# Hybrid decoder layer: the low part of the attention scores on 64-row halves of the array, two key chunks at a time

## The chip, the cores and the metric

The kernel runs on one core of a Trainium2 chip. The metric is the device time of that core in microseconds (us), from several executions of the same program. The lower it is, the better.

## The reference, cut to what matters

The program computes one decoder layer for 2048 tokens of width 1024 in float32. An input norm is followed by one wide projection into queries, keys and values of 4 heads, a convolution branch and two gates. Each head has two query and key vectors of 64 elements per token, and a value of 128. The part that the change touches is the differential attention:

```python
s = jnp.einsum('bhmqd,bhmkd->bhmqk', qb, k).astype(jnp.float32) * scale
s = jnp.where(mask, s, -jnp.inf)
probs = jax.nn.softmax(s, axis=-1)
a = probs[:, :, 0] - lam * probs[:, :, 1]
return jnp.einsum('bhqk,bhkv->bhqv', a.astype(v.dtype), v)
```

After it come the branch outputs, a gated merge, a mixture of 32 experts with two experts per token, and a per-layer embedding. All of these are large matrix products.

## The kernel before, in words

**Number format.** Every operand of a large product is split into a high and a low part (`split`, lines 90 to 93): ScalarE (ACT) rounds the value to the short format, VectorE (DVE) or GpSimd (POOL) subtracts. Ordinary products then take three matmuls, high x high, high x low and low x high (`mm3`, lines 95 to 99). Attention scores are built otherwise. The depth of a score is only 64, so the 128 rows of the array carry the keys' high part in rows 0 to 63 and their low part in rows 64 to 127 (`Kt`, lines 518 to 520), and the query's high part twice, once for each half (`Qt`, slot 2m). One matmul of 128 rows thus gives q-high times (k-high + k-low), and a second one, with the query's low part twice (slot 2m + 1), gives q-low times (k-high + k-low).

**Stages.** `mix` makes the projections and writes q, k, v, gates and the convolution result to scratch in HBM. `attn` follows, then `merge`, `moe` and `ple`. `attn` takes 4 heads times 8 groups of 256 queries. For each group `attn_probs` makes the probabilities, and `attn_out` of the group before multiplies them with the values. Twelve gate columns of `mix` (`mix_gate`, 24 groups of 24 matmuls) are written after the attention in the program, so the scheduler, which orders each engine's instructions by priority at build time, uses them to fill holes of TensorE (PE) in the attention.

**One group of scores.** For each of the two tiles of 128 queries (`qi`) and each of the two softmaxes (`m`) the keys come in chunks of 512. A group g has (2g + 4) // 4 chunks, so 1, 1, 2, 2, 3, 3, 4, 4 for g = 0 to 7. The last chunk is as wide as the causal mask lets it be, at least 256 columns. Per chunk the program takes one of four PSUM banks (`sc`), issues the high matmul (line 582) and the low matmul (line 583), for the last chunk a bf16 matmul that adds the mask (line 585), and then lets DVE find the negative maximum (line 586). ACT takes the exponential (line 572), either chunk by chunk or, where `common` says so, after the maximum over all chunks is known. The probabilities go to tiles `pr` of a ring of `PR_BUFS` = 11 (line 39), a tile for each chunk and query tile, which are released when `attn_out` has transposed them (line 632).

**Loads.** SP's queue brings, at a head's first group, the two `Kt` tiles (lines 519 and 520), the group's `Qt` (lines 526 and 527), and `Vt` (line 530). `Kt` has two buffers, one for each m, so a new head's load waits until the last score of the old head has read them. The gate weights come on the same queue.

**A place elsewhere that the prediction uses.** In `moe`, a block with at most 64 rows of an expert transposes its hidden tile with a stationary operand of 64 rows, and a block with more with one of 128 rows (`turn`, line 1177). Around it stand the products of lines 1131, 1133, 1146 and 1147; those of line 1131 have 64 columns in their stationary operand.

Of the kernel before, what the change touches and what calls it, by code (L numbers as in the profile page):

```python
# [9 lines left out]
F32 = mybir.dt.float32  # L10
# [27 lines left out]
GATES_LATE = 12  # L38
PR_BUFS = 11
QK_AFTER = 10  # L40
# [31 lines left out]
def f32(ap):  # L72
    return ap.bitcast(F32)
# [10 lines left out]
class K:  # L84
# [3 lines left out]

# [1 line left out]
    def split(self, hi, lo, x, lo_eng=None):  # L90
# [43 lines left out]
    def keep(self):  # L134
        """What lasts from the merge to the end."""
        cp = self.ctx.enter_context(self.tc.tile_pool(name="keep", bufs=1, reuse_waits="tile"))
        self.gl = cp.tile([P, NT, NG], F32, name="gl")
        self.nc.vector.memset(self.base, 0.0)
        self.dst = cp.tile([P, NBLK * NE], I32, name="dst")
        self.idx = cp.tile([P, NBLK * NE], I32, name="idx")  # L140
        self.slots = cp.tile([1, 3, NE], I32, name="slots")
        self.xp = self.ctx.enter_context(self.tc.tile_pool(name="xp", bufs=2, reuse_waits="tile"))

    def consts(self, cp):
        nc, A = self.nc, self.A
        cst = cp.tile([P, 4, P], F32, name="cst")
        self.pvt = cp.tile([P, NPV], F32, name="pvt")
        self.bc = cp.tile([P, 36 + 4 * HD], F32, name="bc")
        self.tokm = cp.tile([P, 2 * NT + 1], F32, name="tokm")
        self.maskb = cp.tile([P, P], BF16, name="maskb")  # L150
        self.identb = cp.tile([P, P], BF16, name="identb")
        self.trib = cp.tile([P, P], BF16, name="trib")
        self.ident = cst[:, 0, :]
        self.iota = cst[:, 3, :]
        self.zero = cst[:, 1, :]
        self.base, self.wt, self.tops = (cst[:, 2, a:b] for a, b in ((0, NE), (NE, 2 * NE), (2 * NE, 2 * NE + 3 * NT)))
        self.wt = self.wt.rearrange("p (t k) -> p t k", k=2)
        self.tops = self.tops.rearrange("p (k t) -> p k t", k=3)
        self.onesb = cp.tile([P, P], BF16, name="onesb")
        nc.vector.memset(self.onesb, 1.0)  # L160
        self.st = cp.tile([P, H, NT], F32, name="st")
        self.neglam = cp.tile([P, 1], F32, name="neglam")
        self.s0 = cp.tile([P, H, NT], F32, name="s0")
        self.ones1 = cp.tile([P, 1], F32, name="ones1")
        nc.vector.memset(self.ones1, 1.0)
        self.eps = cp.tile([P, 1], F32, name="eps")
        nc.vector.memset(self.eps, EPS)
        self.qg8 = cp.tile([P, 1], F32, name="qg8")
        # brings in the table of the square root
        nc.scalar.activation(self.neglam, self.ones1, AF.Sqrt)  # L170

        def late():
            nc.sync.dma_start(cst, A["cst"])
            nc.sync.dma_start(self.pvt, A["pv"])
            for to, i in ((self.maskb, 1), (self.identb, 0), (self.trib, 2)):
                nc.vector.tensor_copy(to, cst[:, i, :])
            nc.vector.tensor_scalar_mul(self.qg8, self.pv("qg"), 1.0 / math.sqrt(HD))
            nc.vector.memset(self.zero, 0.0)
            nc.gpsimd.dma_start(self.bc, A["bc"])
            nc.gpsimd.dma_start(self.tokm, A["tokm"])  # L180

        self.late_consts = late

    def rstd(self, pool, ss, shape, n, tag, bufs=None):
        """1 / sqrt(ss / n + eps)."""
        nc = self.nc
# [4 lines left out]

# [1 line left out]
    def mix(self):  # L193
# [109 lines left out]
    def after(self, us, f):  # L303
        """Puts f into the program once the tensor engine has got that much other work."""
        self.todo.append([us, f])
# [18 lines left out]
    def mix_u(self, t0, n, raw=None, also=()):  # L324
        """The normed input of 512 tokens, channels on the partitions, in two parts; raw: where its channels
        may lie; also: what comes between its loads."""
        nc, A, sp, px = self.nc, self.A, self.sp, self.px
# [163 lines left out]

# [1 line left out]
    def attn(self):  # L493
        tc, nc = self.tc, self.nc
        with ExitStack() as ctx:
# [16 lines left out]
            def probs(h, g):  # L512
                if g == 0:
                    self.Kt = []
                    for m in range(2):
                        ms = slice(m * HD, (m + 1) * HD)
                        kt = kp.tile([P, S], F32R, name="Kt", tag="K")
                        for cs in (slice(0, 512), slice(512, S)):
                            nc.sync.dma_start(f32(kt[:HD, cs]), f32(self.KH[h, ms, cs]))
                            nc.sync.dma_start(f32(kt[HD:, cs]), f32(self.KL[h, ms, cs]))  # L520
                        self.Kt.append(kt)
                Qt = kp.tile([P, 4, 256], F32R, name="Qt", tag="Q")
                for l, src in enumerate((self.QH, self.QL)):
# [29 lines left out]
    def attn_probs(self, h, g, Qt, Kt):  # L553
        """Unnormalized p0 - lam * (sum p0 / sum p1) * p1; what is missing, 1 / sum p0, goes into s0."""
        nc, sp = self.nc, self.asp
# [6 lines left out]
        for qi in range(2):  # L562
# [4 lines left out]
            for m in range(2):  # L567
# [7 lines left out]

                for c, w in enumerate(ws):
                    n = max(w, 256)
                    last = c == nch - 1
                    sc = self.pS.tile([P, 512], F32, name="sc", tag="sc")
                    scs.append(sc)  # L580
                    ks = Kt[m][:, c * 512 : c * 512 + n]
                    nc.tensor.matmul(sc[:, :n], Qt[:, 2 * m, qs], ks, start=True, stop=False)
                    nc.tensor.matmul(sc[:, :n], Qt[:, 2 * m + 1, qs], ks, start=False, stop=not last)  # L583
                    if last:
                        nc.tensor.matmul(sc[:, w - P : w], self.identb, self.maskb, start=False, stop=True)
                    nc.vector.tensor_reduce(nm[:, qi, m, c : c + 1], sc[:, :w], AX.X, ALU.max, negate=True)  # L586
                    if not common[m]:
                        exps([c], nm[:, qi, m, c : c + 1])
                if common[m]:
# [57 lines left out]

# [1 line left out]
    def merge(self):  # L649
# [165 lines left out]

# [1 line left out]
    def route(self, q, L):  # L817
# [12 lines left out]
        def first(vals, top, k):  # L830
            """One-hot of the first place that holds the maximum."""
            c, o, i = new(4, k), new(4, k), new(4)
# [57 lines left out]

# [1 line left out]
    def pick(self):  # L892
# [49 lines left out]

# [1 line left out]
    def projected(self, t, pt, w, pool, tag, o):  # L944
        """Tile t of it, from units of [128, 1024] in two parts."""
        for n in range(2):
# [8 lines left out]
    def project(self, parts):  # L955
        """The first half of the tiles, while the table is made."""
        for t, tag in zip(range(0, 8, 2), ("bch", "bcl") * 2):
# [4 lines left out]

# [1 line left out]
    def moe(self):  # L964
# [115 lines left out]
    def unit(self, src, lo_eng=None, after=None):  # L1080
        """A [128, 1024] piece of a weight matrix in two parts."""
        nc = self.nc
# [17 lines left out]
    def turned(self, x, more=False, into=None):  # L1100
        """The transpose of a [128, 1024] tile in two parts, [128, 8, 128] each; `more`: the high part of 64 rows
        once again, right before their low part."""
        nc = self.nc
# [23 lines left out]
    def both(self, ps, x, w, start, stop):  # L1127
        """At most 64 rows: their two parts side by side against the weights' high part."""
        if start:
# [9 lines left out]
    def products(self, w, xt, f, ps, g, i):  # L1139
        """Half of the rows' products with w1 and w3: i = 0, the rows' high part; i = 1, their low part."""  # L1140
        for k in range(4 * g, 4 * g + 4):
# [81 lines left out]
    def weights(self):  # L1223
        """What each of a token's two experts weighs."""
        nc = self.nc
# [11 lines left out]

# [1 line left out]
    def ple(self):  # L1239
# [62 lines left out]
def layout(inputs):  # L1302
    """The inputs as the program reads them: reordered and repeated, never changed."""
    a = {k: np.asarray(v)[0] for k, v in inputs.items()}
# [71 lines left out]
```

## Time and profile before

| | |
|---|---|
| Median of three runs | 2953.11 us |
| The three runs | 2961.81, 2952.98, 2953.11 us |
| Span of the profiled execution | 2960.1 us |
| Time of the profiled execution | 2961.81 us, the only one of the three that is not shorter than the span |
| PE busy | 2736.7 us, 92% of the span |
| DVE, ACT, POOL busy | 69%, 50%, 24% |
| Attention, from its first score to the last | 718 to 1200 us of the span |

The span goes from the first to the last instruction. Some 1.7 us lie around it. Busy times of PE are modelled: a matmul of 512 columns is drawn 0.39 to 0.40 us long, though the next one starts 0.23 us later, so costs of matmuls are read from start to start. PEld is the load of the stationary operand, which can run under the matmul before. "128*128" in a row is rows times columns of the stationary operand, and the shape behind it is that of the moving operand (partitions x columns).

### The profile page before, as it was taken

The page shows a single profiled execution, that of the slowest core. Times are in us where ns is not written, and L with a number is a line of the kernel's source. Part 1 is how long each engine was busy: PE and PEld are TensorE (multiplying, and loading weights), DVE is VectorE, ACT ScalarE, POOL GpSimd, SP SyncE. Part 2 cuts the span into 40 slices and gives each one's busy share as a digit, 9 for nine tenths or more (in the row PEclk, how much of TensorE's full clock was granted, in tenths as well). Part 3 has the DMA queues.
Part 4 walks back from the last instruction along what each step waited for, and adds up shares of the span by engine and source line. Part 5 has one row for each costly group of instructions (what it writes and reads, how often), then busy time and mean ns, then how long its engine had stood idle before and what let it go on. Part 6 is the DMA issues. An engine that isn't in the chain of part 4 may idle for free. (4 is left out here: it accounts for less than half of the span.)

```text
span 2960.1 us, 40065 instructions
## 1 busy us (share of the span) xinstructions
PE 2736.7 (92%) x14078; PEld 2282.7 (77%) x14078; DVE 2041.7 (69%) x2860; ACT 1474.9 (50%) x2712; POOL 722.3 (24%) x463
## 2 busy tenths in 40 slices
PE   7999999999999999999999989898888989888988
PEld 5888877997778788787898867676666767666776
DVE  6995249995878888657567456666667777776564
ACT  4233352335766667544444345555455656565443
POOL 2021130123111000001101134544335444452122
PEclk9999999999999999999999989999999999999999
DMA  5134443235243331456556366777767776876371
GB/s 189 60 107 142 159 147 104 93 114 196 81 132 89 104 112 53 160 184 214 168 170 206 122 238 243 265 287 259 252 223 274 276 283 236 293 274 244 125 246 56
DMA packets 180220, 531.52 MB, mean 180 GB/s; under 512 B 19185, under 2 KB 48641, under 8 KB 179361
## 3 DMA queue, kind: packets, MB, share of 16 engines
q1 hardware_dynamic: 135536, 397.02, 39.9%
q0 software_dynamic: 25904, 92.45, 8.5%
q10 hardware_dynamic: 18432, 37.76, 3.4%
q8 instruction: 177, 2.90, 0.4%
q14 instruction: 171, 1.39, 0.1%
HBM read 424.66 MB, written 102.50 MB: 178 GB/s over the span
## 5 line engine op out<-in xcount | busy, mean ns | idle before, releaser
L93 DVE TENSOR_TENSOR ewl<-eraw,ewh 128x1024 fp32r<-128x1024 f32 x365 | 597.2, 1665 | 94.4 <-ACT ewh L92 88.5
L92 ACT ACTIVATE ewh<-eraw 128x1024 fp32r<-128x1024 f32 x464 | 474.1, 1065 | 54.0 <-PE mps L98 24.9
L387 DVE SCALAR_TENSOR_TENSOR co<-cb,pvt,co 128x1024 f32<-128x1024 f32 x240 | 313.6, 1345 | 1.6
L93 POOL TENSOR_TENSOR ewl<-eraw,ewh 128x1024 fp32r<-128x1024 f32 x99 | 253.8, 2563 | 185.4 <-ACT ewh L92 183.0
L1146 PE MATMUL ups<-ewh,xt 128*128 128x512 f32 x592 | 250.0, 422 | 40.3 <-issue 38.6
L1147 PE MATMUL ups<-ewl,xt 128*128 128x512 f32 x592 | 244.5, 413 | 0.9 <-DVE ewl L93 0.5
L97 PE MATMUL ps<-uh,wh 128*128 128x512 f32 x576 | 232.0, 405 | 4.4 <-ACT uh L92 4.4
L586 DVE TENSOR_REDUCE nm<-sc 128x1 f32<-128x512 f32 (+3 forms) x320 | 185.3, 606 | 66.1 <-PE sc L583 51.6
L98 PE MATMUL ps<-ul,wh 128*128 128x512 f32 x576 | 227.9, 397 | 1.1 <-POOL ul L93 1.1
L99 PE MATMUL ps<-uh,wl 128*128 128x512 f32 x576 | 227.2, 396 | 0.0
L1146 PEld LDWEIGHTS ups<-ewh,xt 128*128 128x128 f32 x592 | 119.0, 201 | 71.9 <-issue 46.0
L97 PE MATMUL ps<-wh,uh 128*128 128x384 f32 x512 | 173.0, 338 | 0.0
L99 PE MATMUL ps<-wh,ul 128*128 128x384 f32 x512 | 172.1, 336 | 0.0
L98 PE MATMUL ps<-wl,uh 128*128 128x384 f32 x512 | 172.0, 336 | 0.0
L1144 PE MATMUL ups<-ewh,xt 128*128 128x512 f32 x592 | 167.5, 406 | 3.7 <-issue 3.7
L97 PE MATMUL mps<-ewh,mh 128*128 128x256 f32 x512 | 150.3, 294 | 4.1 <-ACT mh L92 4.1
L403 POOL DMA_DIRECT2D G<-sg x64 | 35.1, 549 | 457.3 <-ACT sg L402 325.2
L98 PE MATMUL mps<-ewl,mh 128*128 128x256 f32 x512 | 145.8, 285 | 0.0
L99 PE MATMUL mps<-ewh,ml 128*128 128x256 f32 x512 | 145.2, 285 | 0.0
L1147 PEld LDWEIGHTS ups<-ewl,xt 128*128 128x128 f32 x592 | 119.3, 202 | 25.5 <-DVE ewl L93 1.0
L430 POOL TENSOR_TENSOR qn<-qk,qk_std 128x1024 f32<-128x1024 f32 x16 | 44.6, 2785 | 380.7 <-DVE qk_std L189 363.8
L1204 POOL DMA_INDIRECT Y<-y,dst x48 | 72.3, 1507 | 266.3 <-POOLq L1034 188.3
(340 smaller groups left out, 7238.5 us busy)
## 6 DMA issues: line engine op xcount, KB each, us to landing
eraw<-in_we SPq DMA_DIRECT2D x384, 512.0 KB, 7.3
G<-sg POOLq DMA_DIRECT2D x64, 256.0 KB, 2.7
eraw<-in_wac SPq DMA_DIRECT2D x32, 512.0 KB, 4.3
ga<-G SPq DMA_DIRECT2D x32, 512.0 KB, 5.1
eraw<-in_wo SPq DMA_DIRECT2D x32, 512.0 KB, 3.7
ys<-Y SPq DMA_DIRECT2D x32, 512.0 KB, 8.2
wraw<-in_wqkv SPq DMA_DIRECT2D x16, 768.0 KB, 4.2
wraw<-in_wg SPq DMA_DIRECT2D x20, 512.0 KB, 3.9
```

The source lines that it names most:

```text
L92: nc.scalar.activation(hi, x, AF.Copy)
L93: (lo_eng or nc.vector).tensor_tensor(lo, x, f32(hi), ALU.subtract)
L97: nc.tensor.matmul(ps, lh, rh, start=start, stop=False)
L98: nc.tensor.matmul(ps, lh, rl, start=False, stop=False)
L99: nc.tensor.matmul(ps, ll, rh, start=False, stop=stop)
L387: nc.vector.scalar_tensor_tensor(acc, cb[:, i : i + HALF], wi, acc, ALU.mult, ALU.add)
L430: nc.gpsimd.tensor_tensor(qn.rearrange("p t (s d) -> p t s d", d=HD), qk.rearrange("p t (s d) -> p t s d", d=HD), r.unsqueeze(3).to_broadc ...
L586: nc.vector.tensor_reduce(nm[:, qi, m, c : c + 1], sc[:, :w], AX.X, ALU.max, negate=True)
L1144: self.nc.tensor.matmul(ps, xt[1][:, k, :], wk[0], start=False, stop=k == NK - 1)
L1146: self.nc.tensor.matmul(ps, xt[0][:, k, :], wk[0], start=k == 0, stop=False)
L1147: self.nc.tensor.matmul(ps, xt[0][:, k, :], wk[1], start=False, stop=False)
L1204: nc.gpsimd.indirect_dma_start(out=self.Y[:, :], out_offset=bass.IndirectOffsetOnAxis(ap=dst[R], axis=0), in_=y[R], in_offset=None)
```

## The change

The low matmul takes only the keys' high part. It then needs 64 rows, and two chunks are issued as a pair, one on rows 0 to 63 and one on rows 64 to 127. For that the high parts must lie in the other half too: for m = 1 the two halves of `Kt` change places, and a third tile `Kx` holds the high part of m = 0 in rows 64 to 127 and that of m = 1 in rows 0 to 63. `Kx` is loaded by two transfers of 512 KB at each head's start, behind `Kt` and ahead of `Qt`, into one buffer. Its 8 KB per partition are those of two `pr` tiles, so the ring has 9. The order for a pair is now: both high matmuls, both low matmuls, then mask and maxima. A chunk without a partner keeps a low matmul of 128 rows.

```diff
-PR_BUFS = 11
+PR_BUFS = 9
...
                         for cs in (slice(0, 512), slice(512, S)):
-                            nc.sync.dma_start(f32(kt[:HD, cs]), f32(self.KH[h, ms, cs]))
-                            nc.sync.dma_start(f32(kt[HD:, cs]), f32(self.KL[h, ms, cs]))
+                            for r, src in zip((slice(0, HD), slice(HD, P)), (self.KH, self.KL)[:: 1 - 2 * m]):
+                                nc.sync.dma_start(f32(kt[r, cs]), f32(src[h, ms, cs]))
                         self.Kt.append(kt)
+                    kx = kp.tile([P, S], F32R, name="Kx", tag="Kx", bufs=1)
+                    for m in range(2):
+                        nc.sync.dma_start(f32(kx[(1 - m) * HD : (2 - m) * HD]), f32(self.KH[h, m * HD : (m + 1) * HD]))
+                    self.Kt.append([(self.Kt[0], kx), (kx, self.Kt[1])])
...
-                for c, w in enumerate(ws):
-                    n = max(w, 256)
-                    last = c == nch - 1
-                    sc = self.pS.tile([P, 512], F32, name="sc", tag="sc")
-                    scs.append(sc)
-                    ks = Kt[m][:, c * 512 : c * 512 + n]
-                    nc.tensor.matmul(sc[:, :n], Qt[:, 2 * m, qs], ks, start=True, stop=False)
-                    nc.tensor.matmul(sc[:, :n], Qt[:, 2 * m + 1, qs], ks, start=False, stop=not last)
-                    if last:
-                        nc.tensor.matmul(sc[:, w - P : w], self.identb, self.maskb, start=False, stop=True)
-                    nc.vector.tensor_reduce(nm[:, qi, m, c : c + 1], sc[:, :w], AX.X, ALU.max, negate=True)
-                    if not common[m]:
-                        exps([c], nm[:, qi, m, c : c + 1])
+                ns = [max(w, 256) for w in ws]
+                for c0 in range(0, nch, 2):
+                    pair = range(c0, min(c0 + 2, nch))
+                    for c in pair:
+                        n = ns[c]
+                        sc = self.pS.tile([P, 512], F32, name="sc", tag="sc")
+                        scs.append(sc)
+                        nc.tensor.matmul(sc[:, :n], Qt[:, 2 * m, qs], Kt[m][:, c * 512 : c * 512 + n], start=True, stop=False)
+                    for c in pair:
+                        n, r = ns[c], slice(c % 2 * HD, c % 2 * HD + HD)
+                        if len(pair) == 1:
+                            r, ks = slice(0, P), Kt[m]
+                        else:
+                            ks = Kt[2][m][c % 2]
+                        nc.tensor.matmul(scs[c][:, :n], Qt[r, 2 * m + 1, qs], ks[r, c * 512 : c * 512 + n], start=False, stop=c < nch - 1)
+                    for c in pair:
+                        w, sc = ws[c], scs[c]
+                        if c == nch - 1:
+                            nc.tensor.matmul(sc[:, w - P : w], self.identb, self.maskb, start=False, stop=True)
+                        nc.vector.tensor_reduce(nm[:, qi, m, c : c + 1], sc[:, :w], AX.X, ALU.max, negate=True)
+                        if not common[m]:
+                            exps([c], nm[:, qi, m, c : c + 1])
```

## Rows read from the trace of the kernel before

**Rows 1.** The page, busy time of TensorE over the whole span.

```profile
PE 2736.7 (92%) x14078; PEld 2282.7 (77%) x14078; DVE 2041.7 (69%) x2860; ACT 1474.9 (50%) x2712; POOL 722.3 (24%) x463
```

**Rows 2.** Window; busy us of PE, PEld, DVE, ACT, POOL; PEclk, DMA share, GB/s.

```profile
718.00:1200.00 482.00, 464.19 (x2799) 384.26 (x2798) 387.99 (x891) 325.23 (x893) 46.88 (x40) 0.99 0.32 96
```

**Rows 3.** Waits in 718 to 1200 us: total us, times, longest us.

```profile
DVE nm L586 <- PE sc L583: 51.6, 61, 4.6
...
PEld sc L582 <- ACT pr L572: 11.4, 34, 1.7
...
PE po L97 <- DMA Vt<-V: 5.3, 3, 3.4
```

**Rows 4.** Groups by line and shape, 718 to 1200 us: score matmuls.

```profile
L582 PE MATMUL sc<-Kt,Qt 128*128 128x512 f32 x224 | 96.8, 432 | 0.8 <-ACT pr L572 0.5
...
L583 PE MATMUL sc<-Kt,Qt 128*128 128x512 f32 x224 | 89.8, 401 | 0.0
...
L583 PE MATMUL sc<-Kt,Qt 128*128 128x256 f32 x64 | 17.7, 282 | 0.0
...
L583 PE MATMUL sc<-Kt,Qt 128*128 128x384 f32 x32 | 10.8, 345 | 0.0
```

**Rows 5.** Timeline around 1001 us: start us, duration us, instruction.

```profile
1001.07 0.39 PE L582 MATMUL sc<-Kt,Qt 128*128 128x512 f32 x1
1001.07 0.19 PEld L583 LDWEIGHTS sc<-Kt,Qt 128*128 128x128 f32 x1
...
1001.30 0.40 PE L583 MATMUL sc<-Kt,Qt 128*128 128x512 f32 x1
...
1001.53 0.34 PE L582 MATMUL sc<-Kt,Qt 128*128 128x256 f32 x1
...
1001.71 0.28 PE L583 MATMUL sc<-Kt,Qt 128*128 128x256 f32 x1
...
1001.83 0.23 PE L585 MATMUL sc<-maskb,identb 128*128 128x128 bf16 x1
...
1001.87 0.47 PE L582 MATMUL sc<-Kt,Qt 128*128 128x512 f32 x1
...
1002.18 0.39 PE L583 MATMUL sc<-Kt,Qt 128*128 128x512 f32 x1
```

**Rows 6.** Timeline of PE around 744 us: a low matmul of 384 columns.

```profile
744.05 0.34 PE L583 MATMUL sc<-Kt,Qt 128*128 128x384 f32 x1
744.23 0.23 PE L585 MATMUL sc<-maskb,identb 128*128 128x128 bf16 x1
```

**Rows 7.** Timeline around 1833 us: the 64-row transposes of an expert's block.

```profile
1832.70 0.39 PE L1133 MATMUL ups<-ewh,xt 128*128 128x512 f32 x1
1833.01 0.20 PEld L1177 LDWEIGHTS hps<-cst,hd 64*128 64x128 f32 x2 [0.35 <-PE ups L1133]
1833.02 0.34 PE L1177 MATMUL hps<-cst,hd 64*128 64x64 f32 x2
...
1833.28 0.45 PE L1131 MATMUL ups<-ewl,xt 128*64 128x512 f32 x1
...
1833.57 0.40 PE L1133 MATMUL ups<-ewh,xt 128*128 128x512 f32 x1
```

**Rows 8.** Timeline around 1839.5 us: the same transposes with 128 rows.

```profile
1839.35 0.39 PE L1133 MATMUL yd<-ewh,hh 128*128 128x512 f32 x1
...
1839.59 0.38 PE L1177 MATMUL hps<-cst,hd 128*128 128x128 f32 x2
...
1839.72 0.47 PE L1146 MATMUL ups<-ewh,xt 128*128 128x512 f32 x1
...
1840.04 0.40 PE L1147 MATMUL ups<-ewl,xt 128*128 128x512 f32 x1
```

**Rows 9.** All transposes of line 1177: duration ns min/median/max, first and last start, forms.

```profile
L1177 PE MATMUL hps<-cst,hd x196: 221/271/478, 1749.3 to 2706.6; 128*128 128x128 f32 x148, 64*128 64x64 f32 x48
```

**Rows 10.** DMA issues: count, KB each, median us to landing.

```profile
graw<-in_wg SPq DMA_DIRECT2D x12, 512.0 KB, 5.0
```

## The prediction, made before the changed kernel was run

> **What bounds the kernel now.** I began with busy times: PE works 92% of the span, no other engine over 69% [rows 1]. An average hides stages, so I cut out the attention, the only stage that the change touches, from its first score to its last. There PE is busy 464.2 of 482.0 us at a granted clock of 0.99, that is, practically always at the 2.4 GHz level; DVE, the next, is busy 388.0 us [rows 2]. The waits say who is late: DVE waits 51.6 us for the low score matmul, while PE's own waits are small, the largest 11.4 us for a PSUM bank that ACT has yet to read [rows 3]. So PE ends last in this stage, with 17.8 us of idle time (482.0 - 464.2), and its order is full: the gate matmuls have been put into the holes. What PE's work gains or loses here moves the end of the stage, and behind it stands the merge, which cannot start earlier.
>
> Drawn lengths overlap, so I price matmuls from start to start. In the timeline a high matmul of 512 columns is followed 0.23 us later by its low one and that 0.23 us later by the next; a low one of 256 columns takes 1001.83 - 1001.71 = 0.12 us [rows 5], one of 384 takes 0.18 us [rows 6]. The load of the low matmul starts with the high matmul and ends inside it: loads are hidden [rows 5]. Where the matmul ahead is too short to hide one, behind the mask, the next matmul holds the engine 1002.18 - 1001.87 = 0.31 us instead of 0.23: a bare load costs 0.08 us [rows 5].
>
> **The change part by part.**
>
> *Removed: half of the paired low streams.* Per head and m, groups 2 to 7 with two query tiles give (1 + 1 + 1 + 1 + 2 + 2) x 2 = 16 pairs, so 128 in all; 256 of the 320 low matmuls [rows 4] are in pairs. A pair that runs side by side lasts as long as its first chunk, always 512 columns, so the second stream goes: 80 of 512, 16 of 384 and 32 of 256. At most 80 x 0.23 + 16 x 0.18 + 32 x 0.12 = 18.4 + 2.9 + 3.8 = 25.1 us. That is 0.196 us a pair, and so the point from which it pays: everything that a pair adds must stay under it.
>
> *Added: going from 128-row to 64-row matmuls and back, once each a pair.* No score does this now, but the experts' blocks do, in 24 places with two 64-row transposes each [rows 9]. With 128 rows the first transpose starts 1839.59 - 1839.35 = 0.24 us after the matmul ahead, and the matmul behind 0.13 us after the first transpose [rows 8]. With 64 rows these are 1833.02 - 1832.70 = 0.32 and 0.26 us [rows 7]. Going in costs 0.08 us and coming out 0.13, together 0.21. The reason shows in the load: the 64-row one starts only at 1833.01, with its own matmul, 0.31 us after the matmul ahead began; it did not slip under it [rows 7]. 128 x 0.21 = 26.9 us. That alone is as much as is removed.
>
> The Trainium skill (page "TensorEngine Tiling (Array Packing)", section "Key Properties") says the same: a change of the tiling mode, not of the tile alone, makes the TensorE drain. These rows agree, with 0.21 us for both ways; the page gives no figure, and without that rule the sum would be smaller by the 26.9 us and by the bare loads that follow.
>
> *Added: bare loads.* If the switch keeps the load of the first low matmul from running under the high one, it lies open: 0.08 us x 128 = 10.2 us. On the way out the next load is also held. Behind the 64 pairs without a mask that is a 128-column load of a score or filler, 64 x 0.08 = 5.1 us; behind the other 64 it is the mask's short bf16 load, whose successor is bare today already, so I take nothing. The second low matmul has its own load. It may start with the first matmul, as all loads do [rows 5], which lets its stream begin 0.08 us late. That counts where the second chunk is as wide as the first: 80 x 0.08 = 6.4 us. Bounds of the loads: nothing (the transposes carry their load inside the 0.21) to 21.7 us; I take all of it, since in the rows the load and the 64-row matmul start together.
>
> The Trainium skill (page "TensorE: Matmul & The Clock Gate", section "Part 3: Packing small matmuls — row/col tiling") lets matmuls on different rows start about 4 ns after each other. No run here shows it; by it the 6.4 us would shrink to 0.3, and the forecast to 2964.5 us.
>
> *Absorbed.* Of PE's 17.8 us of idle time a part is waiting for ACT and DVE, which a slower PE finds ready. Between 0 and 17.8 us I take a third, 6 us, because the largest single items (a bank, a value tile) are chains through ACT or a DMA [rows 3] that a later PE shortens only in part.
>
> *Reordered: two banks before the first maximum.* The first low matmul now stands behind the second high one, which may wait for its bank. That wait exists now with 11.4 us [rows 3]; the four banks and the exponentials are the same in number. Cost nothing, covered by the gate matmuls; if the order at build time leaves none there, up to another 11.4 us.
>
> *Kx.* Two 512 KB transfers a head, on SP's queue ahead of the new head's Qt. A transfer of that size lands in 5.0 us [rows 10], so Qt comes up to 5 us later, three times (the first head loads under the stage before): 0 to 15 us. While it waits, PE has the last group's value products and gates to do, so I take 0. It waits for the same last scores as Kt[1] does, so SP's queue is held no longer.
>
> *Ring of 9.* A group of four chunks takes 8 tiles, so the run-ahead falls from three chunks to one. ACT and DVE have slack (325 and 388 of 482 us busy [rows 2]); I take 0. The far end is one wait per head of the size of the Vt wait, 4 x 3.4 = 13.6 us [rows 3].
>
> *Sum.* -25.1 + 26.9 + 10.2 + 5.1 + 6.4 - 6 = +17.5 us. The profiled execution took 2961.8 us, 2960.1 of it span, so it would be 2979. It stands 8.7 us over the median of the runs, 2953.1, and the prediction is made against the median: 2970.6 us. Its own range is 2956 (loads half hidden, most waits absorbed) to 2985 (nothing absorbed, a wait at some heads).
>
> **The rivals.** A measurement of this kernel can tell about 0.3%, 9 us, from no change.
>
> *The switch is free for plain matmuls (faster).* Lines 1131 and 1133 change between 64 and 128 columns of the stationary operand and still follow each other at 0.23 us (1833.57 - 1833.28 = 0.29, of which 0.06 is a bare load) [rows 7]; the score loads might likewise slip under the high matmul. Then only the 25.1 us count, of which I let a fifth go to waits that PE now shows, DVE being busy 388 of 457 us: -20 us, 2933 us. It decides as soon as switch and loads stay under 0.196 us a pair. Against it: with 64 rows the 24 places pay.
>
> *Loads hidden, switch paid (no change).* -25.1 + 26.9 = +1.8 us, 2955 us. For it: the 0.21 us already holds the transposes' load. Against it: a 128-column load in front of a 512-column stream has nothing else to lie under.
>
> *The halves do not overlap (slower).* If the second low matmul waits for the first, nothing is removed: 26.9 + 10.2 + 5.1 - 6 = +36 us, 2989 us. No row shows two halves at work at once, so it can't be excluded.
>
> *Qt behind Kx, or the short ring (slower still).* 10 to 15 us on top of the forecast, 2981 to 2986 us; the price is that of the far ends above.
>
> **How the numbers follow.** Forecast 0.50, free switch 0.23, no change 0.14, no overlap 0.07, queue or ring 0.06. I give the forecast half because its main term stands in rows that repeat 24 times, and not more because they are transposes and not scores. Faster by over 0.3%: 0.23. Within: 0.14 and some 0.05 from the low end of the forecast. Slower: the rest, 0.58. The range of 8 in 10 goes from 2930, which takes in the free switch's 2933, to 2988, just short of the case without overlap; what is left out is that case and a gain undiminished by waits.
>
> **What would show it.** Right: in the timeline the first 64-row low matmul starts about 0.32 us after the high one, its load with it; the second starts 0.1 us or less later; what follows the pair starts some 0.4 us after the second instead of 0.23. The attention lasts 15 to 20 us longer with PE still its bound, and DVE waits longer for line 583's successor. Wrong: the low load starts under the high matmul, three starts in a row of 0.23 us or less, and a stage shorter than 482 us; or SP's queue and Qt at the head of PE's waits.

## The result, and the profile after

The changed kernel takes 3073.84 us (median of four runs, 3067.76 to 3074.76) where the kernel before took 2953.34 us on the same chip: a ratio of 1.0389, 95% interval 1.0367 to 1.0411. It is slower by 3.9%, some 115 us by that ratio (the two medians lie 120.5 us apart; gains and losses here go by the ratio). The forecast was slower by 17.5 us; the direction held, the size did not, and the time lies far above the range.

The lines of the scores have moved: the high matmul is now line 588, the low one 596, the mask 600, the maximum 601, the exponential 577, the transposes of the probabilities 647.

First the page (busy times over the whole span), and the window of the attention up to the first product of the merge (busy us of PE, PEld, DVE, ACT, POOL; granted clock, DMA share, GB/s), which answer to [rows 1, 2]; the window of [rows 2] ends just behind the last score, some 24 us ahead of the merge:

```profile
PE 2832.8 (92%) x14078; PEld 2289.8 (75%) x14078; DVE 2051.5 (67%) x2860; ACT 1482.5 (48%) x2712; POOL 718.0 (23%) x463
```

```profile
718.00:1340.00 622.00, 591.01 (x2941) 415.54 (x2940) 411.25 (x915) 343.79 (x912) 45.91 (x42) 0.94 0.29 87
```

The number of matmuls is the same and PE is still the engine that ends last, at 95% of the window. Everything that was lost was lost here: from the first score to the first product of the merge the trace of before has 502.2 us, that of after 615.5 us, 113 more, and what follows takes no longer (1736 us in the trace of before, 1727 after). The waits of 718 to 1340 us (total us, times, longest us) answer to [rows 3]:

```profile
DVE nm L601 <- PE sc L596: 108.6, 141, 5.9
PEld sc L596 <- issue: 59.2, 206, 0.7
PEld sc L588 <- ACT pr L577: 8.1, 26, 1.3
```

DVE waits twice as long for the low matmul as in [rows 3], and the wait for a PSUM bank is no larger. New is the second line: 206 loads of low matmuls that wait for nothing the profile shows. The timeline of PE shows what they are (start us, duration us), beside [rows 5]:

```profile
1059.75 0.39 PE L588 MATMUL sc<-Kt,Qt 128*128 128x512 f32 x1
1060.07 0.50 PE L596 MATMUL sc<-Kx,Qt 64*128 64x512 f32 x1
1060.50 0.39 PE L98 MATMUL po<-al,Vt 128*128 128x256 f32 x1
1060.73 0.40 PE L588 MATMUL sc<-Kt,Qt 128*128 128x512 f32 x1
1061.05 0.49 PE L596 MATMUL sc<-Kt,Qt 64*128 64x512 f32 x1
1061.48 0.23 PE L600 MATMUL sc<-maskb,identb 128*128 128x128 bf16 x1
```

This is a pair of the source, but no pair on the engine. The low matmul of the first chunk runs alone on half of the array, then a value product on all of it, then the second high one and its own low one. PE goes into the 64-row form twice, and no stream is saved. The order of an engine is fixed at build time by what is expected to be ready: the first low matmul needs only the first bank, the second high one another bank, so the low one is put first and a product of another tile between them. I counted over the trace: PE goes into the 64-row form 231 times (a "going" from here on), 206 of them round a single low matmul and only 25 round two.

Where two do stand together, a little later in the same trace:

```profile
1064.53 0.63 PE L588 MATMUL sc<-Kt,Qt 128*128 128x512 f32 x2
1065.09 0.50 PE L596 MATMUL sc<-Kt,Qt 64*128 64x512 f32 x1
1065.10 0.50 PE L596 MATMUL sc<-Kx,Qt 64*128 64x512 f32 x1
1065.53 0.39 PE L588 MATMUL sc<-Kt,Qt 128*128 128x256 f32 x1
1065.75 0.28 PE L596 MATMUL sc<-Kt,Qt 128*128 128x256 f32 x1
```

They start 0.01 us apart, and what follows starts 0.43 us behind the second (1065.53 - 1065.10), just as behind the single one above (1060.50 - 1060.07): the two halves do work side by side, and the second stream costs nothing.

The second thing to see is the end of the stage. One view shows it: the windows of one tile, `gh`, that is, of the gate matmuls which fill PE's holes (two in three of them read it). Columns: length, PE's busy time with these (and their count), granted clock over all, DMA share, GB/s. Before:

```profile
1080.00:1200.00 120.00, 35.96 (x98) 1.00 0.24 75
1200.00:1224.00 24.00, 9.62 (x27) 0.97 0.25 81
```

After:

```profile
1200.00:1224.00 24.00, 5.90 (x17) 1.00 0.17 55
1224.00:1262.00 38.00, 11.09 (x32) 1.00 0.14 43
1262.00:1340.00 78.00, 0.00 (x0) 0.73 0.08 26
```

Before, the gates last to the end of the attention. After, the last one starts at 1257.6 us, 82 us ahead of the merge and 52 us ahead of the last score. In the last 78 us the granted clock is 0.73, that is, part of the time at 1.2 GHz (0.5) and part at 2.4 GHz (1.0). The all-engine windows inside this tail:

```profile
1230.00:1310.00 80.00, 75.24 (x325) 49.49 (x324) 50.78 (x108) 40.62 (x110) 1.08 (x2) 0.85 0.07 21
1310.00:1339.00 29.00, 19.92 (x102) 16.53 (x101) 14.80 (x34) 11.02 (x24) 0.00 (x0) 0.71 0.15 48
```

In the last 29 us PE is busy only 19.9 us: the last groups' chain from score through maximum, exponential, transpose to product lies open, with nothing to put into its holes.

The third is the start. After, PE waits 2.71 us for head 0's `Vt`, whose transfer is issued at 726.60 us where before it was issued at 702.22. Round that wait stands a stretch at a low clock, which began just ahead of it: the clock fell at 731.5 us, the wait lasts from 732.5 to 735.2 us (windows as above; after, then before):

```profile
740.00:760.00 20.00, 19.68 (x61) 11.75 (x59) 9.98 (x27) 10.70 (x30) 4.71 (x2) 0.59 0.27 84
760.00:780.00 20.00, 20.00 (x85) 14.18 (x85) 11.95 (x27) 8.87 (x21) 3.15 (x2) 0.77 0.29 96
```

```profile
740.00:760.00 20.00, 18.85 (x103) 14.22 (x102) 16.78 (x42) 14.29 (x37) 7.70 (x4) 1.00 0.44 133
760.00:780.00 20.00, 19.80 (x116) 16.23 (x116) 15.52 (x38) 15.34 (x46) 3.11 (x2) 1.00 0.17 55
```

PE is busy throughout in both, but after gets 61 matmuls done where before gets 103.

### The profile page after: what moved, and what is told of

The parts are those of the page before. It is cut to its first block, busy times and chain, and to the rows that moved or that the text cites. A ratio compares the mean times of both kernels' runs of the same rounds, so it can differ in the third digit from the quotient of the medians.

```text
span 3066.0 us, 40081 instructions
## 1 busy us (share of the span) xinstructions
PE 2832.8 (92%) x14078; PEld 2289.8 (75%) x14078; DVE 2051.5 (67%) x2860; ACT 1482.5 (48%) x2712; POOL 718.0 (23%) x463
## 5 line engine op out<-in xcount | busy, mean ns | idle before, releaser
L601 DVE TENSOR_REDUCE nm<-sc 128x1 f32<-128x512 f32 (+3 forms) x320 | 191.6, 608 | 143.9 <-PE sc L596 108.6
L1161 PEld LDWEIGHTS ups<-ewh,xt 128*128 128x128 f32 x592 | 118.7, 200 | 68.4 <-issue 42.6
L92 ACT ACTIVATE ah<-tp 128x512 fp32r<-128x512 f32 x144 | 82.4, 597 | 140.1 <-PE tp L647 132.0
L1162 PEld LDWEIGHTS ups<-ewl,xt 128*128 128x128 f32 x592 | 119.1, 201 | 25.1 <-DVE ewl L93 1.0
L1159 PEld LDWEIGHTS ups<-ewh,xt 128*128 128x128 f32 x592 | 113.8, 197 | 28.5 <-issue 4.7
```

The costliest lines, as they stand in the source:

```text
L92: nc.scalar.activation(hi, x, AF.Copy)
L1159: self.nc.tensor.matmul(ps, xt[1][:, k, :], wk[0], start=False, stop=k == NK - 1)
L1161: self.nc.tensor.matmul(ps, xt[0][:, k, :], wk[0], start=k == 0, stop=False)
L1162: self.nc.tensor.matmul(ps, xt[0][:, k, :], wk[1], start=False, stop=False)
```

## The experiments

Twelve kernels, in four groups; those of one group share a chip and the runs of the kernel before. They are told by theme; the number behind each name is its place in the order in which they were run, and "the fourth experiment" is the one with a 4. The medians of the kernel before were 2959.93 us for 1 to 4, 2959.43 for 5 to 7, 2957.87 for 8 to 10, 2962.89 for 11 and 12. Gains and losses in us are the ratio less one times that median, unless another source stands beside them.

### One part at a time

**The ring alone (1).** The kernel before with

```diff
-PR_BUFS = 11
+PR_BUFS = 9
```

> The kernel before with a probability ring of 9 and nothing else. Theory A (the time went to goings between 128-row and 64-row matmuls: the trace after shows 231 of them, 206 around one low matmul and only 25 around a pair): no change, 2953 us within 9. Theory B (the short ring and the Kx loads hold the chain of maxima and exponentials up): 10 to 50 us slower, since B must explain the some 50 us of the 116 us lost in the attention that 231 goings at 0.29 us (67 us) do not.

Measured: 2969.66 us, 1.0038 (1.0019 to 1.0057), +11 us. The ring is not free. The waits of the stage show where most of it may lie; this kernel first, then the one before:

```profile
PEld po L97 <- ACT ah L92: 16.2, 38, 2.2
```

```profile
PEld po L97 <- ACT ah L92: 7.1, 21, 0.8
```

PE waits 9 us longer for the probabilities that the value products read: with two tiles fewer the products follow more closely on what they need.

**The new order alone (2).** The changed kernel with every low matmul on 128 rows; `Kx` is loaded but not read.

```diff
-                        if len(pair) == 1:
+                        if True:
```

> The changed kernel with all low matmuls on 128 rows again, as before the change; its order of high and low matmuls, its ring of 9 and its Kx loads stay (Kx is loaded and not read). Theory A: within 12 us of 2953, no 64-row matmul in the trace. Theory B: 10 to 50 us slower than before, about as much as the ring, the order and Kx cost together in the changed kernel.

Measured: 2973.59 us, 1.0063 (1.0044 to 1.0083), +19 us, of which the ring is 11. That is more than theory A allowed and at the low end of theory B's range; still, order, ring and transfers together are a small part of the 115 us. The bulk is in the 64 rows.

**The price of a going (4).** The kernel before, with its own order, and each low matmul on the first 64 rows, so that the product of the queries' low part with the keys' low part is left out. No stream is saved, so the time is the price of the goings alone.

```diff
-nc.tensor.matmul(sc[:, :n], Qt[:, 2 * m + 1, qs], ks, start=False, stop=not last)
+nc.tensor.matmul(sc[:, :n], Qt[:HD, 2 * m + 1, qs], ks[:HD], start=False, stop=not last)
```

> The kernel before with every low matmul on rows 0 to 63 alone (it leaves out q-low times k-low, as the change does); no pairs, no Kx, ring of 11. Theory A: 318 goings at 0.29 us are +92 us of TensorE work, so at least 3030 us, and up to 3110 if what follows from a program order made for other lengths grows as in the changed kernel (116 for 67 us). Theory B: the goings alone cost less than their length, below 3020 us, since the ring is long and SP's queue as before.

Measured: 3053.87 us, 1.0344 (1.0304 to 1.0383), +102 us (90 to 113) by the ratio and +94 by the medians. In the traces the stage grows from 502.2 to 596.5 us, by 94, so I take 94. The trace has 319 goings: 94 / 319 = 0.295 us each. Its timeline and its largest wait of PE's loads:

```profile
1000.28 0.36 PE L582 MATMUL sc<-Kt,Qt 128*128 128x256 f32 x1
1000.57 0.38 PE L583 MATMUL sc<-Kt,Qt 64*128 64x256 f32 x1
1000.89 0.38 PE L97 MATMUL po<-ah,Vt 128*128 128x256 f32 x1
```

```profile
PEld sc L583 <- issue: 68.7, 259, 0.4
```

The low matmul starts 0.29 us after a high one of 256 columns, and the next matmul 0.32 us after it. With 128 rows these two steps are 0.18 and 0.12 us [rows 5]. The granted clock over this stage (718 to 1320 us) is 0.98, so goings by themselves do not bring it down. PE is idle for 11.0 us of it (602.00 - 591.00), where before it was idle for 20.8 (506.00 - 485.21 in 718 to 1224 us): some 10 us of the goings were absorbed by what had been waits, so 0.295 us is a net price; without that a going would come to some 0.33 us (104 / 319).

**Half as many (10).** The same for m = 0 only, 160 low matmuls and 159 goings in the trace, the same product left out there.

```diff
-nc.tensor.matmul(sc[:, :n], Qt[:, 2 * m + 1, qs], ks, start=False, stop=not last)
+r = slice(0, P if m else HD)
+nc.tensor.matmul(sc[:, :n], Qt[r, 2 * m + 1, qs], ks[r], start=False, stop=not last)
```

> The kernel before with the low matmuls of the first softmax (m = 0) alone on rows 0 to 63, the others on 128 rows; it leaves out q-low times k-low for m = 0. With all of them 318 goings cost 94 us, 0.295 us each. If the price is linear: 160 goings, 47 us slower (40 to 55). If TensorE's idle time takes up the first of them: below 35 us.

Measured: 3005.94 us, 1.0156 (1.0114 to 1.0198), +46 us (34 to 59), and the stage in the trace is 46 us longer: 46 / 159 = 0.29 us each. As far as the intervals tell, the price is linear in the number of goings, so it may be multiplied by 231.

**The gates alone (5).** The kernel before, with the gate columns written into the loop over the groups so early that none stands behind the 600th of the 640 score matmuls.

```diff
+EARLY_TO = 0.87
...
+                done = sum(g + 1 for _, g in groups[: n + 1])
+                while len(late) < GATES_LATE and (len(late) + 1) / GATES_LATE * EARLY_TO <= done / (H * 36):
+                    j = 16 - GATES_LATE + len(late)
...
+                    self.mix_gate(j, HALF, late[j], self.u)
```

> The kernel before (ring of 11, 128-row low matmuls, no Kx), with its gate columns put earlier into the program, so that TensorE's order has none left behind the 600th of 640 score matmuls, as in the changed kernel; in the kernel before they last to the end. Theory C (beside the price of the goings, the changed kernel loses time because its build-time order has used up the gates, and the attention's end runs without anything to fill its waits): 10 to 45 us slower than before, with long gaps of TensorE and a lower granted clock only in the last part of the attention. Rival D (the waits come from pairs and ring all along the attention): within 9 us of before.

Measured: 2982.40 us, 1.0076 (1.0054 to 1.0097), +22 us. Its last windows have the same signs as those of after, idle time and a fallen clock:

```profile
1162.00:1223.00 61.00, 53.28 (x288) 42.74 (x286) 48.22 (x102) 38.23 (x106) 1.08 (x2) 0.92 0.07 24
1223.00:1252.00 29.00, 20.91 (x124) 17.07 (x123) 15.89 (x35) 12.19 (x27) 0.00 (x0) 0.84 0.11 31
```

The end of the kernel before, of about the same length:

```profile
1135.00:1194.00 59.00, 58.98 (x351) 49.05 (x349) 49.53 (x110) 39.43 (x109) 1.64 (x3) 1.00 0.12 38
1194.00:1224.00 30.00, 27.02 (x172) 23.00 (x171) 15.80 (x36) 14.04 (x30) 1.62 (x3) 0.98 0.23 74
```

PE's idle time in these windows is 15.8 us against 3.0, and what the clock is short of full adds up to 9.5 us against 0.6: 21.7 us more in all. So 22 us can be lost at the end without a single 64-row matmul.

### The pairs as the source means them

**Held together (3).** The changed kernel with each low matmul of a pair ordered behind the second high one, and given priority, so that nothing comes between. In the trace 124 of the 128 pairs now stand side by side.

```diff
...
+                        with ExitStack() as near:
+                            if len(pair) == 2:
+                                near.enter_context(self.tc.high_priority(200))
+                            low = nc.tensor.matmul(scs[c][:, :n], Qt[r, 2 * m + 1, qs], ks[r, c * 512 : c * 512 + n], start=False, stop=c < nch - 1)
+                        if len(pair) == 2:
+                            self.behind(low, high)
...
```

> The changed kernel with its pairs held together: a low matmul may be ordered only behind the second high one, and has a higher priority, so that 124 of 128 pairs stand next to each other in TensorE's program. Theory A, with the trace's prices for an adjacent pair (in 0.33 instead of 0.23 us, the two 0.003 us apart, out 0.43 instead of 0.23 us): per pair 0.09 + 0.20 - 0.23 = +0.06 us where the second chunk has 512 columns, +0.11 with 384, +0.17 with 256, so 80 x 0.06 + 16 x 0.11 + 32 x 0.17 = +12 us: about 2965 us, at most 2985. Theory B: still over 3000 us, because ring and Kx are as in the changed kernel.

Measured: 3017.19 us, 1.0211 (1.0177 to 1.0245), +62 us. Half of the loss is gone, so the splitting was worth some 53 us (115 - 62), but the forecast's +12 is missed by far: theory A fell here, and the number is on B's side.

```profile
1021.41 0.65 PE L588 MATMUL sc<-Kt,Qt 128*128 128x512 f32 x2
1021.99 0.18 PEld L599 LDWEIGHTS sc<-Kx,Qt 64*128 64x128 f32 x1 [0.30 <-issue]
1021.99 0.50 PE L599 MATMUL sc<-Kx,Qt 64*128 64x512 f32 x1
1021.99 0.18 PEld L599 LDWEIGHTS sc<-Kt,Qt 64*128 64x128 f32 x1
1021.99 0.44 PE L599 MATMUL sc<-Kt,Qt 64*128 64x384 f32 x1
1022.42 0.23 PE L605 MATMUL sc<-maskb,identb 128*128 128x128 bf16 x1
```

The pair itself does as planned: both loads and both streams at once, and the mask 0.43 us after them. What stands beside it is this, in its waits and in its last window:

```profile
PEld sc L588 <- ACT pr L577: 27.4, 69, 1.3
```

```profile
1254.00:1283.00 29.00, 18.43 (x103) 14.94 (x101) 15.62 (x36) 11.68 (x25) 0.00 (x0) 0.77 0.16 53
```

The wait for a bank has gone from 11.4 us [rows 3] to 27.4, and the gates are used up at 1224.7 us, 58 us ahead of the end.

**Gates spread (6).** The same, with each half gate column issued behind the first score of a group, evenly over the stage.

```diff
...
+                    with tc.issue_after(mark.ins):
+                        self.mix_gate(j, HALF, late[j], self.u, (n,))
...
```

> The kernel with the pairs held together (2.1% slower than before), and its gates held back: each half of a gate column may be ordered only behind the first score of a group, evenly over the attention, so that gates are left to the end. Theory C: the end runs as the rest does; left are 19 us of ring, order and Kx and 12 us of the goings, so 25 to 40 us slower than before (ratio 1.008 to 1.014). Rival D: still 50 to 65 us slower, because the waits do not sit at the end.

Measured: 3009.58 us, 1.0172 (1.0137 to 1.0207), +51 us. A miss: 11 us back where 22 or more were expected, and the intervals overlap, so even the 11 are not certain; the number falls to rival D. The end itself is mended: in the last 91 us PE is idle for 8.0 us instead of 15.5, and the clock is short of full by 2.4 us instead of 10.4. But the stage in the trace is only 7 us shorter (554.2 against 561.5), so about half of what the end gained is lost ahead of it, where the gates were taken from.

**Ring of 11 (7).** The pairs held together, `PR_BUFS` = 11 again, and the room taken from two buffers of the gate weights (3 to 2 each).

> The kernel with the pairs held together, with the ring of 11 again; the 8 KB come from the gate weights, whose high and low parts get 2 buffers instead of 3. TensorE's order still has hardly any gate behind the 600th score matmul. Theory C: gates run out as before, so 40 to 60 us slower than before. A rival E (the short ring is what makes the tail): 12 to 25 us slower than before, the goings and Kx alone.

Measured: 3006.73 us, 1.0150 (1.0116 to 1.0184), +44 us.

**Both (9).** Spread gates and the ring of 11.

> Pairs held together, gates held back to the end of the attention, ring of 11 (gate weights in 2 buffers instead of 3), Kx as in the change. Ring and tail are gone, left are the goings around 124 pairs and Kx. By the trace a going costs 0.094 us in, 0.196 out and 0.105 for the bare load of the matmul behind it (0 where a mask follows), against a saved stream: +0.16 us for 64 pairs without a mask, +0.06, +0.11 and +0.17 for the 16, 16 and 32 with one, together +18 us. Additive account: 18 to 30 us slower than before. If pairs in themselves bring waits that the account does not have: 40 us or more.

Measured: 3003.41 us, 1.0164 (1.0124 to 1.0204), +48 us. By the times, whichever of the two is applied first, the second brings nothing that can be told. The stages in the traces, 561.5 us with neither cure, 554.2 with spread gates, 550.1 with the ring and 545.8 with both, do nearly add up. What remains, +48 us by the ratio (35 to 60) and 44 in the stage (545.8 - 502.2), is the loss of the idea with its pairs intact. The waits:

```profile
PEld sc L597 <- ACT pr L586: 23.4, 64, 1.7
DVE nm L615 <- PE sc L608: 95.6, 71, 5.2
```

Counting the matmuls' own waits of the same kind too, PE and its loads wait 30.5 us for banks here and 13.5 in before. Part of a load's wait passes under the matmul ahead of it: PE's whole idle time grows by less, from 20.8 to 31.9 us (550.00 - 518.15 in 718 to 1268 us). A pair takes two of the four banks at once and gives neither to DVE before both low matmuls are through, which would explain both lines; no run changed it.

### `Kx` and the start

**Order without `Kx` (8).** The second experiment, with no `Kx` at all.

> The changed kernel's order of high and low matmuls and its ring of 9, with 128-row low matmuls and without Kx at all. The ring alone cost 0.38% (11 us), ring, order and an unread Kx 0.63% (19 us). If Kx is what lies between, this run is 8 to 14 us slower than before; if the order is, 15 to 22 us.

Measured: 2973.78 us, 1.0049 (1.0029 to 1.0069), +14 us. By time this can't be told from the 1.0063 with `Kx`. The traces differ clearly at the start: without `Kx` head 0's `Vt` is issued at 702.85 us, as before, and the first 80 score matmuls take 48.8 us as against 48.7 before; they take 53.3 us in the second experiment, with an unread `Kx`, and 60 to 70 us in the kernels that read it. Not all of the latter is `Kx`: the fourth experiment, without it, takes 59.3 us there, by its goings.

**`Kx` behind `Vt` (11 and 12).** Two kernels, the best pairs and the changed kernel itself, with the tile asked for at the same place and its two transfers moved behind those of `Qt` and `Vt`. (The expectation says "allotted and loaded behind"; only the loads were moved.)

```diff
-                    for m in range(2):
-                        nc.sync.dma_start(f32(kx[(1 - m) * HD : (2 - m) * HD]), f32(self.KH[h, m * HD : (m + 1) * HD]))
...
+                    for m in range(2):
+                        nc.sync.dma_start(f32(kx[(1 - m) * HD : (2 - m) * HD]), f32(self.KH[h, m * HD : (m + 1) * HD]))
```

> The kernel with pairs held together, gates held back and the ring of 11 (48 us slower than before), with Kx allotted and loaded behind Vt instead of ahead of Qt. In all kernels with Kx the first head's Vt starts at 724 to 727 us instead of 702, TensorE waits some 3 us for it, and the granted clock is 0.8 instead of 0.96 over the first 60 us, which cost 12 us there. If that is Kx's place: Vt starts near 702 again, and the run is 33 to 40 us slower than before. If the start of Vt does not move: 44 us or more.

> The changed kernel as it is, with Kx allotted and loaded behind Vt instead of ahead of Qt. It lost 115 us, 19 of them in the first 68 us, where the clock was at 0.75. If Kx's place is their cause: 95 to 105 us slower than before. Otherwise 110 us or more.

Measured: 3007.54 us, 1.0153 (1.0127 to 1.0180), +45 us, and 3070.84 us, 1.0379 (1.0349 to 1.0408), +112 us. Neither moved. SP's queue and PE in the first of them:

```profile
727.63 0.34 SPq L532 DMA_DIRECT2D Vt<-V  x1
728.02 1.10 SPq L534 DMA_DIRECT2D Kx<-KH  x2
737.61 0.55 PE L97 MATMUL po<-ah,Vt 128*128 128x256 f32 x1 [3.75 <-DMA Vt<-V]
```

`Vt` is now ahead of `Kx` and still goes out at 727.6 us. So it isn't held by `Kx` on the queue. What it does wait for stands among the waits of SP's queue in the trace of after (695 to 732 us):

```profile
SPq L535 <- DMA CT<-co: 17.6, 3, 15.2
```

`CT<-co` writes the convolution's result of the stage before to scratch. A wait for it ahead of head 0's `Vt`, 14.6 to 20.2 us long at a stroke, stands in all eight kernels with `Kx` and in none of the six without. The two transfers have no tensor in common, so this fits a `Vt` that is given the memory of `co`, since `Kx` has taken another place; but other places were not tried, and that part stays open.

## Why the prediction was wrong

**Bound.** Right. PE ends the stage in every kernel, and the time follows what its order gains or loses.

**Removed: 25.1 us.** Wrong for the changed kernel, by its premise that a pair of the source is a pair on the engine. Only 25 pairs stood together, so 25 x 0.196 = 5 us were saved.

**Added: going in and out, once each a pair. This is the step that failed.** The price was right, in part by luck, the number was not. From start to start over the whole trace a low matmul of 64 rows starts 0.33 us behind the high one instead of 0.23 (+0.09; I had 0.08 and a bare load of 0.08), what follows starts 0.43 us behind it instead of 0.23 (+0.20; I had 0.13 and, without a mask, 0.08), and the matmul after that has its load bare, +0.1, unless it is the mask. So going in with its load was put too high and coming out too low, and the errors met. The runs give 0.295 us per going for all of it, where the terms of switch and first load had 0.21 + 0.08 = 0.29. But there are 231 goings instead of 128. The signs that I had named, 0.32 us, 0.1 us or less and 0.4 us in the timeline, came true wherever a pair stands; they could not show how many stand. With 231 in place of 128 the two terms of switch and bare load alone would have come to 231 x 0.29 = 67 us instead of 37.

The Trainium skill (page "TensorEngine Tiling (Array Packing)", section "Key Properties") says that a change of the tiling mode drains the engine. The fourth and the tenth experiment agree, with 0.29 us per going as the price of one such round trip.

**Bare load of the second low matmul: 6.4 us.** Should have been 0: in the held pairs both loads start at 1021.99 us, with both streams. The Trainium skill (page "TensorE: Matmul & The Clock Gate", section "Part 3: Packing small matmuls — row/col tiling"), whose 4 ns I cited and did not take, agrees with the 0.01 us or less that these rows show; the trace of before could not settle it.

**Absorbed: 6 us.** Right in kind where the gates last to the end: 10 us in the fourth experiment. Not seen in the changed kernel, where PE is idle for 31.0 us (622.00 - 591.01) against 20.8 before: it uses up the gates early and finds less to do at the end.

**Reordered: cost nothing, covered by the gate matmuls. The second step that failed.** I named the cover and not its size. A PE that fills more holes per score runs out of gates: they end 52 us ahead of the last score and 82 us ahead of the merge, and the fifth experiment, where they end 71 us ahead of the merge, prices this at 22 us. With the pairs held together the bank wait that I had put at 0 to 11.4 us shows as well, at up to 17 us over before (30.5 - 13.5).

**Kx: nothing.** The mechanism was another. `Qt` is hardly late (one wait of 0.55 us at head 0); head 0's `Vt` is, and the clock round it is low. In 740 to 780 us the clock is short of full by 0.41 x 20 + 0.23 x 20 = 12.8 us. That is read from the trace and no run of the changed kernel undid it; that `Vt` brings it about is not shown, since the clock fell before PE waited.

**Ring of 9: nothing.** 11 us, near its far end.

**Sum.** 231 x 0.295 = 68, less 5 for the streams saved, plus 22 at the end, 11 for the ring and 13 at the start: 109 us. Measured are 113 us in the stage and 115 us (108 to 121) by the ratio. The terms are from separate kernels and may overlap, so the agreement to 6 us is better than it deserves. The 22 us above all is borrowed: read as in the fifth experiment, the end of the changed kernel itself (1230 to 1339 us) has 13.8 us of idle time and 20.4 us of missing clock, 31 more than before, with which the sum would be 118.

With the pairs intact the sum is: 124 pairs at 0.29, half of them with 0.1 more, less 0.196 saved, so about 0.15 x 124 = 18 us; bank waits 17; the start 12 (60.3 us for the first 80 scores against 48.7): 47 us, where the kernel with spread gates and the ring of 11 measured 48 by the ratio and 44 in its stage. Apart from the price of a going, these terms are read from its trace and were not undone one by one, and they overlap: the first 80 scores hold 13 of the pairs, some 2 us, and 6.3 us of the bank waits. So the 47 may be some 8 us too high. The forecast's "+17.5 with PE as the bound" is close to what the pairs themselves cost by this account, the 18 us, which no run shows alone, and what went wrong is what they do to the order round them.

**The rivals.** The free switch is refuted by the fourth experiment, hidden loads by the same 0.295 us, halves that don't overlap by the 0.01 us between their starts, `Qt` behind `Kx` by the last two kernels, where moving `Kx` behind changed nothing. The short ring, priced with it at 10 to 15 us, did come true with its 11. That the change doesn't do what it says, which I did not price, was the one that came true: on the engine most pairs were not pairs.

**What is open.** Whether `Vt` goes out late because of the place that it has in memory; how much of the clock's low stretch at the start is its doing; how much of the second experiment's +19 us is `Kx` and how much the order, since 1.0049 and 1.0063 overlap; and how much of the 44 us with intact pairs is waiting for banks. No kernel that was run beats the one before; the best with pairs loses 44 us.

## What to carry to other kernels

Count the mode changes in the order that the engine runs, not in the source: where a scheduler orders by readiness, two matmuls written next to each other part as soon as one of their inputs is ready first. A stay in the 64-row form costs about 0.29 us here, more than a stream of 512 columns (0.23), so it has to save at least two such streams, and a pair saves one. Work that fills holes is a stock: for every hole that a change adds, ask whether the stock lasts to the end of the stage.

## What was not expected of the hardware

At the head of the attention the granted clock of the changed kernel fell from 2.4 to 1.2 GHz twice, at 731.5 and at 752.0 us, and stayed there for 17.1 us each time. Ahead of the first fall PE was busy 3.09 of 6.00 us (725 to 731 us); the wait of 2.71 us for `Vt` came only after it. Ahead of the second PE was busy 11.94 of 13.00 us (735 to 748) and 3.00 of 3.00 (749 to 752), and during it all of 17.00 us (752 to 769). The kernel before has the first fall too, at 731.2 us, after 3.44 busy of 6.00 us, but for 3.4 us only, and no second. Between 720 and 790 us the clock is low for 17 to 34 us in the eight kernels whose `Vt` is late and for 3.4 to 10.2 us in the other six. So a late `Vt` goes together with a longer low stretch; why, and why a busy PE got the low clock a second time, is not settled.
